# Expert layers: scatter by transposed one-hots, weighing a step ahead of combining, two groups gathered at once; swiglu with the input halves side by side

## The chip, the cores and the metric

One NeuronCore of a Trainium2 chip runs the whole program in one launch. The metric is the device time in microseconds. The kernel before takes 2146.79 us, the median of three runs (2145.88 to 2148.48).

## The reference

Two blocks follow one another, all in fp32, with 256 latent tokens and 256 context tokens of 1024 channels. The first block has two layers, each an attention and Fourier mixer and an expert layer. The second block has one layer: a mixer of two scans, and a swiglu of width 2816.

```python
def expert_choice_ffn(h, w_router, w_gate_e, w_up_e, w_down_e):
    B, N, _ = h.shape
    cap = CAPACITY_FACTOR * N // N_EXPERTS                       # 2 * 256 // 16 = 32
    aff = jax.nn.softmax((h @ w_router).astype(jnp.float32), axis=-1)
    top_aff, top_idx = lax.top_k(aff.transpose(0, 2, 1), cap)    # each expert picks 32 tokens
    bidx = jnp.arange(B)[:, None, None]
    xg = h[bidx, top_idx]
    a = jnp.einsum("becd,edf->becf", xg, w_gate_e)               # 16 experts, 1024 -> 1024
    u = jnp.einsum("becd,edf->becf", xg, w_up_e)
    out = jnp.einsum("becf,efd->becd", jax.nn.silu(a) * u, w_down_e) * top_aff[..., None]
    return jnp.zeros_like(h).at[bidx, top_idx].add(out)

def swiglu(h, w_gate, w_up, w_down):
    return (jax.nn.silu(h @ w_gate) * (h @ w_up)) @ w_down
...
x = x + g2[:, None, :] * expert_choice_ffn(h, w_router[l], w_gate_e[l], w_up_e[l], w_down_e[l])
if need_ctx:                                                     # layer 0 only
    xc = xc + cg2[:, None, :] * expert_choice_ffn(hc, w_router[l], w_gate_e[l], w_up_e[l], w_down_e[l])
```

Layer 0 sends two sets of tokens (latents and context) through its experts, layer 1 one set.

## The kernel before

**Expert layers.** `moe` runs a layer in steps e = 0 to 16. Step e issues `up(e)` (gate and up of expert e, eight loads of 1 MB), the activation, `down(e-1)` (four loads of 1 MB), the transposes `turn(e)`, and then what tables name for that step. The 192 loads of a layer are issued by SyncE, whose queue is in order. They go through a ring of SBUF buffers, and a load waits until TensorE is done with what the buffer held before; it also waits for the load eight before it. All ring buffers bear the name `we` in the rows, and a buffer that leaves the ring keeps that name. `LEAVE` says at which load number a buffer leaves, and `big()` then hands it out to hold other data. The ring of layer 0 shrinks in this way from 19 buffers to 10 at load 92, that of layer 1 from 18 to 5.

The 16 experts are four groups of four. The tokens of a group are gathered by matrix products of the tokens (`xr`) with one-hot matrices `P`: `route` returns `gather(g, k)`, which handles channel block k (of 8) of group g for each set, and writes a 128x128 result per set through ScalarE or VectorE into `xg`. `GATHER` puts the gathers of groups 1, 2 and 3 into steps 3, 5 and 7. The way back is prepared by `scatter_mats` at step 7 (`SCATTER`): for each group and set, two products with selection constants (`cscat`) spread the positions `pos` and affinities `affT` over 128 partitions, and two VectorE operations make the matrix `PT` and the weights `aff` from them, through one PSUM buffer. `combine(g)` at steps 7, 9, 12 and 16 (`COMBINE`) weighs the group's outputs by `aff`, splits them into a high and a low half (`oh`), and multiplies them by `PT`. `moe` writes its calls in this order, but a scheduler interleaves the instructions of each engine by priority; `behind()` lets what is in it start no earlier than what has been issued so far.

**Layer 1** carries side work for the second block: its first projections for the context (`hc,w`, `w,hc`), whose loads share SyncE's queue.

**Swiglu.** For fp32 accuracy a product is done as three products of halves (`mm3`): high by high, high by low, low by high. The inputs are split once (`hl`), the weights per block of 256 columns: `halves` casts on ScalarE (`whi`, L173) and subtracts on VectorE (`wlo`, L174), each in two pieces of 1024 columns. Each of the 11 blocks has gate and up (for each, two column halves j and eight kk, so 48 matmuls 256 wide), tanh, two products, a split, and down (24 matmuls 512 wide).

Of the kernel before, what the change touches and what calls it, by code (L numbers as in the profile page):

```python
# [9 lines left out]
F32 = mybir.dt.float32  # L10
F32R = mybir.dt.float32r
# [8 lines left out]
E = 16  # L20
# [67 lines left out]
def _const_scatter():  # L88
    i = np.arange(128)
    sel4 = np.zeros((128, 2, 4, 128))  # L90
    for s in range(2):
        for g in range(4):
            sel4[s * 16 + 4 * g + i // 32, s, g, i] = 1
    return _pack([("p32", (i % 32)[:, None]), ("sel4", sel4)])
# [18 lines left out]
LEAVE = [dict(B=[44, 68, 68, 20, 20], A=[92] * 4), dict(A=[68, 92, 92, 20, 20], S=[32] * 4, O=[32] * 4)]  # L113
# [4 lines left out]
GATHER = {3: 8, 5: 8, 7: 8}  # L118
# [4 lines left out]
class Kernel:  # L123
# [727 lines left out]
    def route(self, l, S):  # L851
# [7 lines left out]
        aff = rp.tile([128, 2, S, E], F32, name="aff")  # L859
# [10 lines left out]
        self.affT = self.ep.tile([R, 256], F32, name="affT")  # L870
        nc.scalar.copy(self.affT, pt.rearrange("p t n -> p (t n)"))
# [20 lines left out]
        def pick(g):

            for s in range(S):
                P[s] = ep.tile([128, 2, 4, 32], F32, name="P1", bufs=2 * S)
                for t in range(2):
                    nc.vector.tensor_tensor(P[s][:, t], iota, pT[:, t, s, 4 * g:4 * g + 4].unsqueeze(2)
                                            .to_broadcast([128, 4, 32]), op=OP.is_equal)
                    nc.vector.tensor_scalar(P[s][:, t], P[s][:, t], r[:, 2 * s + t:2 * s + t + 1], None, op0=OP.mult)

        def gather(g, k):
            if k == 0:
                pick(g)
            ps = self.psum("pg" if g else "mm", [128, S, 4, 32])
            for s in range(S):
# [1062 lines left out]
```

## Time and profile before

| | |
|---|---|
| median of three runs | 2146.79 us |
| profiled execution: time, span | 2146.93 us, 2145.2 us |
| TensorE busy | 1891.1 us (88%) |
| VectorE, ScalarE busy | 969.2 us (45%), 546.9 us (25%) |
| read from HBM | 598.84 MB, mean 280 GB/s over the span |
| expert loads | 3 x 128 of 1024 KB, median 14.4, 12.2 and 14.4 us from issue to landing |
| mean granted TensorE clock | 0.927 |

The table is an average over stages with different limits. The slices of the span, the windows over single stages and the queue that issues the loads tell more, and the rows below are taken from those.

### The profile page before, as it was taken

What the parts mean: (1) busy time and instruction counts of PE and PEld (TensorE: products, weight loads), DVE (VectorE), ACT (ScalarE), POOL (GpSimd) and SP (SyncE); (2) the same over time, 40 slices, a digit from 0 to 9 for tenths busy, and PEclk for the clock granted to TensorE, in tenths of its full rate; (3) what the DMA queues carried; (4) which work ended last, traced back from release to release, by engine and by line L of the source; (5) the groups of instructions that cost most, each with busy time, mean ns of one, the idle gap of its engine ahead of it and who ended that gap; (6) DMA issues with size and microseconds to landing.
All of it is one profiled execution on the core that took longest, in us unless ns stands there. A gap on an engine that the chain in (4) does not pass through costs nothing. (4 is left out here: it accounts for less than half of the span.)

```text
span 2145.2 us, 31259 instructions
## 1 busy us (share of the span) xinstructions
PE 1891.1 (88%) x13102; PEld 1266.5 (59%) x13102; DVE 969.2 (45%) x1928; ACT 546.9 (25%) x1076; POOL 75.4 (4%) x97
## 2 busy tenths in 40 slices
PE   5989999997999998887899977688876669998998
PEld 3957778894443432223878953354432228897997
DVE  3875668743222332215776632222121037765454
ACT  4144532221011100003354410210100024344342
POOL 0210000000000000000200000000000000100000
PEclk9999999998999999999999988798787769998999
DMA  8755738745999789997315579999899983213451
GB/s 317 276 210 204 280 137 344 305 191 225 394 420 420 314 322 419 421 421 299 116 60 206 198 298 416 419 388 394 365 420 415 419 365 118 99 68 130 177 180 57
DMA packets 85453, 601.93 MB, mean 281 GB/s; under 512 B 10048, under 2 KB 10848, under 8 KB 13376
## 3 DMA queue, kind: packets, MB, share of 16 engines
q1 hardware_dynamic: 82928, 594.15, 69.7%
q10 hardware_dynamic: 1840, 5.46, 0.7%
q8 instruction: 103, 1.69, 0.3%
q0 software_dynamic: 544, 0.32, 0.2%
q14 instruction: 38, 0.31, 0.0%
HBM read 598.84 MB, written 1.05 MB: 280 GB/s over the span
## 5 line engine op out<-in xcount | busy, mean ns | idle before, releaser
L158 PE MATMUL ps<-we 128*32 128x256 f32 (+2 forms) x2400 | 356.5, 526 | 85.5 <-DMA we<-w_up_e_dram 41.2
L158 PEld LDWEIGHTS ps<-we 128*32 128x32 f32 (+2 forms) x2400 | 122.5, 137 | 298.0 <-issue 114.7
L174 DVE TENSOR_TENSOR wlo<-w,whi 128x1024 fp32r<-128x1024 f32 x170 | 205.3, 1220 | 94.3 <-ACT whi L173 93.8
L173 ACT CAST whi<-w 128x1024 fp32r<-128x1024 f32 x170 | 174.2, 1045 | 234.8 <-PE ps L164 142.5
L158 PE MATMUL ps<-we,gT 128*32 128x256 f32 (+1 forms) x1536 | 203.6, 502 | 31.0 <-DMA we<-w_down_e_dram 31.0
L1037 DVE TENSOR_TENSOR we<-ps,we 32x512 f32<-32x512 f32 (+1 forms) x128 | 70.9, 554 | 212.5 <-PE ps L158 202.3
L158 PEld LDWEIGHTS ps<-we,gT 128*32 128x32 f32 (+1 forms) x1536 | 66.3, 127 | 141.9 <-issue 74.4
L163 PE MATMUL ps<-hhi,whi 128*128 128x512 f32 (+1 forms) x384 | 131.3, 342 | 0.1
L164 PE MATMUL ps<-hlo,whi 128*128 128x512 f32 (+1 forms) x384 | 131.3, 342 | 0.0
L165 PE MATMUL ps<-hhi,wlo 128*128 128x512 f32 (+1 forms) x384 | 129.5, 340 | 0.1
L158 PE MATMUL ps<-we,xg 128*32 128x256 f32 (+1 forms) x768 | 100.4, 486 | 5.3 <-DMA we<-w_gate_e_dram 3.7
L1004 DVE TENSOR_TENSOR g<-tanh,ps 128x512 f32<-128x512 f32 (+1 forms) x32 | 17.7, 554 | 186.3 <-PE ps L158 186.2
L163 PE MATMUL ps<-hl,whi 128*128 128x256 f32 x352 | 100.7, 286 | 0.1
L165 PE MATMUL ps<-hl,wlo 128*128 128x256 f32 x352 | 99.8, 285 | 0.0
L164 PE MATMUL ps<-hl,whi 128*128 128x256 f32 x352 | 99.7, 285 | 0.0
L1001 ACT ACTIVATE tanh<-ps 128x512 f32<-128x512 f32 (+1 forms) x32 | 15.7, 490 | 309.7 <-PE ps L158 309.7
L164 PE MATMUL ps<-wlo,hhi 128*128 128x256 f32 x320 | 91.7, 288 | 1.0 <-DVE wlo L174 1.0
L165 PE MATMUL ps<-whi,hlo 128*128 128x256 f32 x320 | 91.7, 290 | 0.3 <-DVE hlo L371 0.3
L163 PE MATMUL ps<-whi,hhi 128*128 128x256 f32 x320 | 91.4, 287 | 0.3 <-ACT whi L173 0.3
L1002 DVE SCALAR_TENSOR_TENSOR tanh<-tanh,ps 128x512 f32<-128x512 f32 (+1 forms) x32 | 17.7, 555 | 163.0 <-ACT tanh L1001 162.8
L158 PEld LDWEIGHTS ps<-P,xr 128*128 128x128 f32 x384 | 52.4, 203 | 59.5 <-issue 27.4
L1012 ACT ACTIVATE gT<-ps 128x512 f32<-128x512 f32 (+1 forms) x32 | 15.7, 490 | 278.5 <-PE ps L169 278.5
(425 smaller groups left out, 3500.8 us busy)
## 6 DMA issues: line engine op xcount, KB each, us to landing
we<-w_gate_e_dram SPq DMA_DIRECT2D x128, 1024.0 KB, 14.4
we<-w_up_e_dram SPq DMA_DIRECT2D x128, 1024.0 KB, 12.2
we<-w_down_e_dram SPq DMA_DIRECT2D x128, 1024.0 KB, 14.4
w<-w_in_dram SPq DMA_DIRECT2D x53, 1024.0 KB, 5.2
w<-w_ada_dram SPq DMA_DIRECT2D x48, 1024.0 KB, 6.0
w<-w_mod_dram SPq DMA_DIRECT2D x24, 1024.0 KB, 6.5
w<-w_out_dram SPq DMA_DIRECT2D x12, 1024.0 KB, 5.6
w<-w_gate_dram SPq DMA_DIRECT2D x11, 1024.0 KB, 4.8
```

The lines of the kernel that those rows point to most:

```text
L158: self.nc.tensor.matmul(ps, l, r, start=first, stop=last)
L163: mm(ps, l[0], r[0], start=first, stop=False)
L164: mm(ps, l[0], r[1], start=False, stop=False)
L165: mm(ps, l[1], r[0], start=False, stop=last)
L173: self.nc.scalar.copy(hi, x)
L174: (eng or self.nc.vector).tensor_tensor(lo, x, hi.bitcast(F32), op=OP.subtract)
L1001: nc.scalar.activation(t, pa[:, :W], AF.Tanh, scale=0.5)
L1002: nc.vector.scalar_tensor_tensor(t, t, 1.0, pa[:, :W], op0=OP.add, op1=OP.mult)
L1004: nc.vector.tensor_tensor(g, t, pu[:, :W], op=OP.mult)
L1012: nc.scalar.activation(gT[e], ps, AF.Copy, scale=0.5)
L1037: nc.vector.tensor_tensor(op[e // 4 % 2][p:p + 32, s, j * W:j * W + W], ps[i, :W], gb[s][i, j * W:j * W + W], op=OP.mult)
```

## The change

In `route`, the one-hots of all groups are kept unscaled (`hot`), and `scaled` makes the scaled matrix `P` for the gather from them. A gather can handle n = 2 groups at once, with a 256 wide `P`. `GATHER` becomes {3: 8, 5: 4, 6: 4}: group 1 alone in step 3, groups 2 and 3 together in steps 5 and 6. One buffer of layer 0 leaves the ring at load 68 and no longer at 92.

`scatter_mats` transposes the one-hots (`ident,hot`) in place of the products with `cscat`, copies them from PSUM by ScalarE and VectorE in turn, and gets the affinities by a product of the one-hots with the softmax (`aff,hot`, 4 columns wide). `combine` is cut in two: `weigh` stays at its step, and the matrix products move into the next step.

In the swiglu the two halves of the input lie side by side (`hx`), so that the high half of a weight is multiplied with both by one matmul 512 wide. The low half of a weight is multiplied with the high half of the input as before. The two halves of the result are added by a ScalarE copy and a VectorE addition for each column half j, and the activation reads that sum (`fspg`, `fstp` in the rows) from SBUF.

```diff
-LEAVE = [dict(B=[44, 68, 68, 20, 20], A=[92] * 4), dict(A=[68, 92, 92, 20, 20], S=[32] * 4, O=[32] * 4)]
+LEAVE = [dict(B=[44, 68, 68, 20, 20], A=[68, 92, 92, 92]), dict(A=[68, 92, 92, 20, 20], S=[32] * 4, O=[32] * 4)]
-GATHER = {3: 8, 5: 8, 7: 8}
+GATHER = {3: 8, 5: 4, 6: 4}
...
+        hot = self.hot = [ep.tile([128, 2, E, 32], F32, name="hot", bufs=S) for _ in range(S)]
+        def pick(g, n):
+            e = slice(4 * g, 4 * g + 4 * n)
...
+                    nc.vector.tensor_tensor(hot[s][:, t, e], iota, pT[:, t, s, e].unsqueeze(2)
+                                            .to_broadcast([128, 4 * n, 32]), op=OP.is_equal)
+        def scaled(g, n):
...
+                    nc.vector.tensor_scalar(P[s][:, t], hot[s][:, t, 4 * g:4 * g + 4 * n],
+                                            r[:, 2 * s + t:2 * s + t + 1], None, op0=OP.mult)
...
+        def gather(g, n, k):
...
+            ps = self.psum("pg" if g else "mm", [128, S, n, 4, 32])
             for s in range(S):
                 for t in range(2):
                     self.mm(ps[:, s], self.X[s][:, t, k * 128:k * 128 + 128],
                             P[s][:, t].rearrange("p e c -> p (e c)"), t == 0, t == 1)
...
+                for i in range(n):
+                    put(g + i, k, s, ps[:, s, i])
...
     def scatter_mats(self, S, big):
...
-                ps = self.psum("sm", [128, 2, 256])
-                self.mm(ps[:, 0], sel4[:R, s, g], self.pos, True, True)
-                self.mm(ps[:, 1], sel4[:R, s, g], self.affT, True, True)
-                nc.vector.tensor_scalar(self.PT[:, g, s], ps[:, 0], self.const("p32"), None, op0=OP.is_equal)
-                j = self.eq.tile([128, 256], F32, name="affj")
-                nc.vector.scalar_tensor_tensor(j, ps[:, 1], 1.0, self.PT[:, g, s].bitcast(F32), op0=OP.mult,
-                                               op1=OP.mult, accum_out=self.aff[:, g, s:s + 1])
+                ps = self.psum("tp", [128, 2, 128])
+                for t in range(2):
+                    h = self.hot[s][:, t, 4 * g:4 * g + 4].rearrange("p e c -> p (e c)")
+                    self.tr(ps[:, t], h)
+                    self.mm(pa[:, g, s], h, self.probs[:, t, s, 4 * g:4 * g + 4], t == 0, t == 1)
+                (nc.vector.tensor_copy if (g + s) % 2 else nc.scalar.copy)(self.PT[:, g, s],
+                                                                         ps.rearrange("p t n -> p (t n)"))
+        own = ep.tile([128, 4 * S, 4], F32, name="affj")
+        nc.vector.tensor_tensor(own, pa.rearrange("p g s e -> p (g s) e"),
+                                self.const("of4").unsqueeze(1).to_broadcast([128, 4 * S, 4]), op=OP.mult)
+        nc.vector.tensor_reduce(self.aff.rearrange("p g s -> p (g s)"), own, axis=AX, op=OP.add)
...
+            if e - 1 in COMBINE:
+                combine(COMBINE.index(e - 1), range(S))
             if e in COMBINE:
-                combine(COMBINE.index(e))
+                g = COMBINE.index(e)
+                for sets in ([range(S)] if g < 3 else [[s] for s in range(S)]):
+                    weigh(g, sets)
+                    if g == 3:
+                        combine(g, sets)
...
-                    ps = self.psum(tag, [128, 2, 256])
+                    s = p.tile([128, 2, 256], F32, name="fs" + tag, bufs=2)
                     for j in range(2):
+                        ps = self.psum(tag, [128, 2, 256])
                         for kk in range(KT):
-                            self.mm3(ps[:, j], [x[:, kk, j * 128:j * 128 + 128] for x in w], [h[:, kk] for h in hl],
-                                     kk == 0, kk == KT - 1)
+                            l = [x[:, kk, j * 128:j * 128 + 128] for x in w]
+                            nc.tensor.matmul(ps, l[0], hx[:, kk], start=kk == 0, stop=False, skip_group_check=True)
+                            nc.tensor.matmul(ps[:, 0], l[1], hx[:, kk, 0], start=False, stop=kk == KT - 1,
+                                             skip_group_check=True)
+                        nc.scalar.copy(s[:, j], ps[:, 1])
+                        nc.vector.tensor_tensor(s[:, j], s[:, j], ps[:, 0], op=OP.add)
```

What this moves on the engines is seen at three places. The first is TensorE in layer 0 around step 7. Before, the products with `cscat` and the first `combine` (`we 128x512`) stand between the end of the gather (`P,xr`) with `down(6)` (`we,gT`) and `up(8)` (`we 64x512`):

```order
L158 MATMUL ps<-we,gT 64x512 x4
L158 MATMUL ps<-P_5600,xr 128x128 x2
L158 MATMUL ps<-pos,cscat 128x256
L158 MATMUL ps<-affT,cscat 128x256
L158 MATMUL ps<-pos,cscat 128x256
L158 MATMUL ps<-affT,cscat 128x256
L158 MATMUL ps<-we 128x512 x6
L158 MATMUL ps<-pos,cscat 128x256
L158 MATMUL ps<-affT,cscat 128x256
L158 MATMUL ps<-we 128x512 x4
```

In the changed kernel, the transposes (`ident,hot`) and the 4-wide products (`aff,hot`) stand inside `down(6)` and the start of `up(8)`, and the first `combine` inside `down(7)`:

```order
L154 MATMUL ps<-aff,hot 128x4 x10
L165 MATMUL ps<-ident,hot 128x128 x2
L154 MATMUL ps<-aff,hot 128x4 x3
L154 MATMUL ps<-we,gT 64x512 x12
L154 MATMUL ps<-we 64x512 x4
L165 MATMUL ps<-ident,hot 128x128 x8
L154 MATMUL ps<-we 64x512
L165 MATMUL ps<-ident,hot 128x128 x2
L154 MATMUL ps<-we 64x512 x27
L165 MATMUL ps<-ident,g 128x128 x4
L154 MATMUL ps<-we,gT 64x512 x4
L154 MATMUL ps<-we 128x512 x5
```

The whole of `up(8)` has moved ahead of the first `combine`, and no gather stands in step 7 any more. The second place is SyncE's queue in layer 1. Before, a load of the second block's `w_in` (`w_12398`) stands between two loads of expert 8's `up`:

```order
L800 DMA we<-w_gate_e_dram 128x2048 x4
L800 DMA we<-w_up_e_dram 128x2048
L1184 DMA w_12398<-w_in_dram 128x2048
L800 DMA we<-w_up_e_dram 128x2048 x3
L800 DMA we<-w_down_e_dram 128x2048 x4
```

In the changed kernel it stands behind the last expert load, with the other loads of `w_in`:

```order
L796 DMA we<-w_up_e_dram 128x2048 x4
L796 DMA we<-w_down_e_dram 128x2048 x8
L1205 DMA w_12315<-w_small_dram 128x384
L1205 DMA w_12317<-w_in_dram 128x2048
L1205 DMA w_12319<-w_in_dram 128x2048
L1205 DMA w_12321<-w_in_dram 128x2048
L1205 DMA w_12323<-w_in_dram 128x2048
L1205 DMA w_12325<-w_in_dram 128x2048
L1205 DMA w_12327<-w_in_dram 128x2048
L1205 DMA w_12329<-w_in_dram 128x2048
```

One load of 1 MB has left the stream of layer 1. The third place is ScalarE in the swiglu, over one block. Before:

```order
L1828 ACTIVATE ft<-ps 128x512
L173 CAST whi<-w 128x1024 x2
L1833 ACTIVATE fghi<-fy 128x512
L173 CAST whi<-w 128x1024 x4
L1828 ACTIVATE ft<-ps 128x512
```

In the changed kernel, where `fspg` and `fstp` are the sums of gate and up:

```order
L1851 COPY fspg<-ps 128x256
L169 CAST whi<-w 128x1024
L1856 ACTIVATE ft<-fspg 128x512
L1851 COPY fstp<-ps 128x256
L169 CAST whi<-w 128x1024
L1851 COPY fstp<-ps 128x256
L169 CAST whi<-w 128x1024
L1861 ACTIVATE fghi<-fspg 128x512
L169 CAST whi<-w 128x1024 x2
L1851 COPY fspg<-ps 128x256
```

Four copies a block stand between the casts that split the weights.

## Rows read from the trace of the kernel before

**Rows 1.** The page, part 2, mean GB/s of the 40 slices of 53.6 us.

```profile
GB/s 317 276 210 204 280 137 344 305 191 225 394 420 420 314 322 419 421 421 299 116 60 206 198 298 416 419 388 394 365 420 415 419 365 118 99 68 130 177 180 57
```

**Rows 2.** The page, part 4, the chain that ended last, share by engine.

```profile
PE 25%; DMA 10%; DVE 3%; issue 3%; ACT 1%; POOL 0%; DVEq 0%; POOLq 0%; ACTq 0%; SPq 0%
```

**Rows 3.** Windows: us, busy PE, PEld, DVE, ACT, POOL, clock, DMA share, GB/s.

```profile
720.00:760.00 40.00, 36.73 (x140) 18.84 (x142) 18.43 (x41) 5.33 (x10) 0.00 (x0) 0.83 0.47 181
```

**Rows 4.** SyncE's queue, 737 to 761 us: start, us, the issues merged.

```profile
737.11 23.33 SPq L800 DMA_DIRECT2D we<-w_down_e_dram  x2
```

**Rows 5.** Waits of SyncE's queue, 700 to 780 us: total, times, longest.

```profile
SPq L800 <- PE ps L158: 53.9, 19, 22.6
```

**Rows 6.** TensorE in order, layer 0: start, us, operation, idle before.

```profile
740.95 1.22 PE L158 MATMUL ps<-pos,cscat 32*128 32x256 f32 x2 [2.18 <-DVE affj L933]
...
759.00 1.94 PE L158 MATMUL ps<-we 128*64 128x512 f32 x8
```

**Rows 7.** Groups by shape, 700 to 770 us: busy, mean ns, idle before.

```profile
L158 PE MATMUL ps<-P,xr 128*128 128x128 f32 x64 | 10.8, 296 | 2.3 <-ACT we L914 1.3 <-DVE we L911 0.9
...
L158 PE MATMUL ps<-we 128*128 128x512 f32 x16 | 7.7, 616 | 0.3 <-DVE xr L1058 0.3
L158 PE MATMUL ps<-pos,cscat 32*128 32x256 f32 x16 | 7.1, 528 | 2.2 <-DVE affj L933 2.2
L158 PE MATMUL ps<-affT,cscat 32*128 32x256 f32 x16 | 5.7, 438 | 0.0
```

**Rows 8.** TensorE, fp32 matmuls 256 wide, two records to each.

```profile
1426.06 7.07 PE L158 MATMUL ps<-w,hc 128*128 128x256 f32 x32
```

**Rows 9.** TensorE, transposes of 128 columns.

```profile
610.90 0.66 PE L169 MATMUL ps<-ident,g 128*128 128x128 f32 x4
```

**Rows 10.** TensorE, fp32 matmuls 8 wide, two records to each.

```profile
1510.18 1.06 PE L158 MATMUL ps<-da,cscan 128*128 128x8 f32 x8
```

**Rows 11.** Window in layer 1, columns as in rows 3.

```profile
1480.00:1520.00 40.00, 35.46 (x263) 20.97 (x262) 12.91 (x32) 4.76 (x11) 0.00 (x0) 0.76 0.77 313
```

**Rows 12.** SyncE's queue, layer 1.

```profile
1484.03 0.42 SPq L1184 DMA_DIRECT2D w<-w_in_dram  x1
1506.86 2.69 SPq L800 DMA_DIRECT2D we<-w_up_e_dram  x3
```

**Rows 13.** Groups of TensorE by shape, 1464 to 1508 us.

```profile
L158 PE MATMUL ps<-hc,w 128*128 128x256 f32 x32 | 9.4, 465 | 0.0
L158 PE MATMUL ps<-P,xr 128*128 128x128 f32 x32 | 6.0, 304 | 2.6 <-DVE we L911 1.5 <-ACT we L914 1.1
...
L158 PE MATMUL ps<-pos,cscat 16*128 16x256 f32 x8 | 3.8, 568 | 1.1 <-DVE affj L933 1.1
```

**Rows 14.** Window behind layer 1, columns as in rows 3.

```profile
1760.00:1768.00 8.00, 4.31 (x18) 3.15 (x19) 4.15 (x11) 4.87 (x10) 1.41 (x2) 0.54 0.42 178
```

**Rows 15.** Window of the swiglu, columns as in rows 3.

```profile
1944.00:2134.00 190.00, 189.89 (x1326) 177.58 (x1326) 96.14 (x106) 73.97 (x88) 0.00 (x0) 0.99 0.41 145
```

**Rows 16.** TensorE in the swiglu: start, us, operation.

```profile
2003.80 0.28 PE L165 MATMUL ps<-hl,wlo 128*128 128x256 f32 x1
...
2005.23 0.28 PE L165 MATMUL ps<-hl,wlo 128*128 128x256 f32 x1
2005.35 0.40 PE L163 MATMUL ps<-whi,fghi 128*128 128x512 f32 x1
...
2006.05 0.40 PE L163 MATMUL ps<-whi,fghi 128*128 128x512 f32 x1
```

**Rows 17.** Groups of the swiglu by shape: busy, mean ns, idle before.

```profile
L174 DVE TENSOR_TENSOR wlo<-w,whi 128x1024 fp32r<-128x1024 f32 x60 | 72.3, 1222 | 66.7 <-ACT whi L173 66.6
...
L173 ACT CAST whi<-w 128x1024 fp32r<-128x1024 f32 x60 | 61.4, 1043 | 100.0 <-PE ps L164 50.1 <-PE ps L165 28.6 <-issue 21.3
...
L1828 ACT ACTIVATE ft<-ps 128x512 f32<-128x512 f32 x11 | 6.5, 593 | 3.8 <-PE ps L165 3.8
...
L371 DVE TENSOR_TENSOR hl<-hf,hl 128x256 fp32r<-128x256 f32 x5 | 2.1, 426 | 0.2
```

More of the change, by code (lines that the diff above doesn't have):

```diff
@@ L89, in _const_scatter @@
     i = np.arange(128)
[L90 to L94, printed above, removed]
+    return _pack([("of4", i[:, None] // 32 == np.arange(4)[None, :])])
 def _const_scan():
@@ L879, in route @@
         nc.vector.tensor_scalar(sel, wk, 0.0, None, op0=OP.is_lt)
-        self.pos = self.ep.tile([R, 256], F32, name="pos")
         nc.vector.tensor_tensor_scan(wk, sel, sel, 0.0, op0=OP.add, op1=OP.max)
-        nc.vector.tensor_tensor(self.pos, wk, sel, op=OP.mult)
-        nc.vector.tensor_scalar(self.pos, self.pos, -1.0, None, op0=OP.add)
+        nc.vector.tensor_tensor(wk, wk, sel, op=OP.mult)
+        nc.vector.tensor_scalar(wk, wk, -1.0, None, op0=OP.add)
         pt = self.psum("sm", [128, 2, S, E])
@@ L901, in gather @@
-        def gather(g, k):
+                    nc.vector.tensor_tensor(hot[s][:, t, e], iota, pT[:, t, s, e].unsqueeze(2)
+                                            .to_broadcast([128, 4 * n, 32]), op=OP.is_equal)
+        def scaled(g, n):
+            for s in range(S):
+                P[s] = ep.tile([128, 2, 8, 32], F32, name="P1", bufs=2)[:, :, :4 * n]
+                for t in range(2):
+                    nc.vector.tensor_scalar(P[s][:, t], hot[s][:, t, 4 * g:4 * g + 4 * n],
+                                            r[:, 2 * s + t:2 * s + t + 1], None, op0=OP.mult)
@@ L902, in gather, with put @@
+        def put(g, k, s, ps):
+            o = self.xg[g][:, k, :, s]
+            if (k + s + g) % 2:
+                nc.vector.tensor_scalar(o, ps, coef[0][:, k, s:s + 1], coef[1][:, k, s:s + 1], op0=OP.mult, op1=OP.add)
+            else:
+                nc.scalar.activation(o, ps, AF.Identity, scale=coef[0][:, k, s:s + 1], bias=coef[1][:, k, s:s + 1])
+        def gather(g, n, k):
             if k == 0:
-                pick(g)
-            ps = self.psum("pg" if g else "mm", [128, S, 4, 32])
+                pick(g, n)
+                scaled(g, n)
+            ps = self.psum("pg" if g else "mm", [128, S, n, 4, 32])
@@ L992, in up @@
                     if gather and i == 0:
-                        gather(0, k)
+                        gather(0, 1, k)
                     for j in range(J):
@@ L1038, in down, with weigh @@
                                             gb[s][i, j * W:j * W + W], op=OP.mult)
-        def combine(g):
-            end = g == 3
+        def weigh(g, sets):
             if g == 0:
                 oh.extend(big(F32R).rearrange("p (s d) -> p s d", s=S) for _ in range(2))
-            for s in range(S):
+            for s in sets:
                 o, hi, lo = op[g % 2][:, s], oh[0][:, s], oh[1][:, s]
@@ L1050, in combine @@
                                                    op0=OP.mult, op1=OP.subtract)
+        def combine(g, sets):
+            end = g == 3
+            for s in sets:
+                hi, lo = oh[0][:, s], oh[1][:, s]
                 for h in range(2):
@@ L1065, in moe @@
         ups = up(0, gather)
-        self.consts(eq, _const_scatter, "cscat", 1 + 512 * S)
-        rest = iter(range(KT, 4 * KT))
+        self.consts(eq, _const_scatter, "cscat")
+        rest = iter([(1, 1, k) for k in range(KT)] + [(2, 2, k) for k in range(KT)])
         for e in range(E + 1):
@@ L1077, in moe @@
             for _ in range(GATHER.get(e, 0)):
-                x = next(rest)
-                if x % KT == 0:
-                    self.xg.append(big().rearrange("p (k e s c) -> p k e s c", k=KT, e=4, s=S))
-                gather(x // KT, x % KT)
+                g, n, k = next(rest)
+                if k == 0:
+                    self.xg.extend(big().rearrange("p (k e s c) -> p k e s c", k=KT, e=4, s=S) for _ in range(n))
+                gather(g, n, k)
             if e == 2:
@@ L1645, in block2 @@
         hp = self.st.enter_context(self.pool("eh", side="left"))
-        room = lambda dtype: [hp.tile([128, KT, 256], dtype, name="hl", tag=x) for x in ("hi", "lo")]
-        hl = room(F32)
+        h = hp.tile([128, 2, KT, 256], F32, name="hl", tag="h")
+        hl = [h[:, 0], h[:, 1]]
         self.queue(["small", 0, 256, 2080, 2336, 2592, 512, 768, 1024, 1280, 1568, 1824, -1, -2, -3, -4],
@@ L1667, in block2 @@
         self.dbg("x2", xs[0])
-        self.swiglu(xs, r, room(F32R))
+        self.swiglu(xs, r, hp.tile([128, KT, 2, 256], F32R, name="hx", tag="h"))
     def mix2(self, p, xs, hl):
@@ L1793, in scans, with swiglu @@
         return o
-    def swiglu(self, xs, r, hl):
+    def swiglu(self, xs, r, hx):
         nc, a, m = self.nc, self.a, self.modT[2]
@@ L1814, in swiglu @@
             for fb in range(F // 256):
-                pss = []
+                sums = []
                 for n, tag in (("w_gate_2", "pg"), ("w_up_2", "tp")):
```

36 lines of the change are left out of this document (11 added, 25 removed).

## Prediction

> **What bounds the kernel now.** I read the slices of the span first. In the expert layers the transfer rate has a roof of about 420 GB/s: it stands at 419 to 421 for slices on end [rows 1]. The chain that ended last goes through TensorE for 25% of the span and through DMA for 10% [rows 2], so where the layers wait, they wait for weights. Time is lost where the rate falls below the roof inside an expert layer. Slices 14 and 15 (layer 0) show 314 and 322, a loss of (106 + 98) / 420 x 53.6 = 26.0 us of transfer. Slices 27 to 29 (layer 1) show 388, 394 and 365, a loss of (32 + 26 + 55) / 420 x 53.6 = 14.4 us [rows 1]. The first and last slices of a layer are mixed with other stages and are left out.
>
> Then I looked for the place. In layer 0 the window of 720 to 760 us moves 181 GB/s [rows 3], which is 239 / 420 x 40 = 22.8 of the 26.0 us. SyncE issues one load at 737.11 and the next at 760.11 (the row's last issue begins 0.33 us before its end) [rows 4], and the longest wait of its queue is 22.6 us, for TensorE [rows 5]. The ring holds 10 buffers there and a layer's first load of `up(8)` is number 8 + 7 x 12 = 92, so load 102 waits until `up(8)` is done with its first buffer. TensorE comes to it only at 759.00 [rows 6]. In layer 1 the ring holds five: load 97 waits for load 92. The window of 1480 to 1520 us moves 313 GB/s [rows 11], a loss of 107 / 420 x 40 = 10.2 us, and SyncE stands from 1484.03 to 1506.86 [rows 12]. The swiglu is bound otherwise: TensorE is busy 189.89 of 190 us at a granted clock of 0.99 [rows 15].
>
> **The change, part by part.** The sums go against the profiled execution's 2146.93 us, 0.14 us from the median.
>
> *Layer 0, ahead of `up(8)`.* Between 700 and 770 us TensorE spends 10.8 us on group 3's gather and idles 2.3 us for its evacuation; 7.1 and 5.7 us on the two selection products of the scatter, with 2.2 us of idle time for the one PSUM buffer (2.18 us of it in one row [rows 6]); and 7.7 + 0.3 us on `combine(0)` [rows 7]. Six of the eight pairs of the scatter stand ahead of `up(8)`: 12.8 x 6/8 + 2.2 = 11.8. So 13.1 + 11.8 + 8.0 = 32.9 us stand in the way. In their place come at most 16 transposes at 0.66 / 4 = 0.165 us [rows 9] and 16 narrow products at 1.06 / 4 = 0.265 us [rows 10], 6.9 us. The double gather has 8 x 4 = 32 matmuls of 256 columns at 7.07 / 16 = 0.442 us [rows 8], 14.1 us, where group 2 alone took about the 13.1 us of group 3: 1.0 us more. Net, TensorE is at `up(8)` some 32.9 - 6.9 - 1.0 = 25 us earlier, at about 735 us, before load 101's issue of old.
>
> That removes the wait that ends last there. Late next are the loads behind `up(7)` and `down(6)`, since steps 5 and 6 now hold the gathers of two groups and the ring still has only 10 buffers; I leave 4 us of the 26.0 there and take a gain of 22 us. Bounds: 26 if nothing is left, and 13 if the 13.1 us of group 3's gather come back as a stall two steps earlier. The earlier leave of one buffer (load 68 for 92) changes the ring from 14 to 13 where the rows show no loss. From there to the end of the layer TensorE is hidden under the transfers (slices 16 to 18 stand at 419 to 421 [rows 1]), so what the stream gains the layer ends earlier. The 16 copies from PSUM are shared by ScalarE and VectorE, which were busy 5.33 and 18.43 of 40 us [rows 3].
>
> *Layer 1, ahead of `up(8)`.* The gather goes (6.0 + 2.6 us), and the `pos` products (3.8 + 1.1 us) with those for the affinities, of the same count and width; eight transposes and eight narrow products come (3.4 us), which I set against the affinity products [rows 13]. That is 13.5 us, and `combine(0)` on top, against 10.2 us lost: all of it should come back. What stays ahead of `up(8)` is the context's projection, 9.4 us [rows 13]. Of the other 4.2 us of the layer's loss I take 2, since part comes from the gather in step 5, which is now longer. Gain 12 us, bounds 8 and 14.4.
>
> *The load that leaves layer 1.* One load of 1.05 MB at 420 GB/s is 2.5 us of that stream. It now comes behind the layer, where the window of 1760 to 1768 us moves 178 GB/s [rows 14] and has room for 242 x 8 = 1.9 MB. I take 2 us; bounds 0 and 2.5.
>
> *Swiglu, TensorE.* Twelve steps of 256 columns take 2003.80 to 2005.23, 0.119 us each; three of 512 take 2005.35 to 2006.05, 0.233 us each [rows 16]. Three of the first are 0.3575 us, one of each is 0.3525: 352 x 0.005 = 1.8 us less. Bounds: 2.8 us less if each 256 columns cost half a 512 step (0.1165 us), and nothing. [...]
>
> *Swiglu, the other engines.* Added are 44 ScalarE copies of 256 columns. ScalarE takes 0.593 us for 512 and 1.043 for 1024 columns [rows 17], so 0.45 less per 512 and about 0.37 for 256: 16.3 us. Added are 44 VectorE additions at 0.426 us [rows 17], 18.7 us. ScalarE goes from 73.97 to about 90 and VectorE from 96.14 to about 115 of 190 us [rows 15], so TensorE covers both on average, and I cost them at nothing. If the cover is gone, a late split costs TensorE a cast and a subtraction, 1.04 + 1.22 = 2.27 us [rows 17].
>
> *The start of a layer* gets one or two VectorE operations ahead of the first gather, 0.3 us in all, with the 0.426 us of rows 17 as the nearest price and 0 to 1 as bounds; the gathers of the later groups lose as many.
>
> Sum: 22 + 12 + 2 + 1.8 - 0.3 = 37.5 us, so 2146.9 - 37.5 = 2109 us.
>
> **The rivals.**
>
> *The stall moves.* The double gathers stand in steps 5 and 6, in front of loads that the same short ring holds back. For it: SyncE's queue waited 19 times for TensorE between 700 and 780 us, not once [rows 5]. Against it: the sum of TensorE's work before `up(8)` falls by 25 us, wherever the gathers stand. Then the lower bounds hold: 13 + 8 + 0 + 0 = 21 us, 2126 us.
>
> *The splits of the swiglu come late.* ScalarE's queue is in program order in the trace, and a copy that waits for TensorE's column half keeps the casts behind it waiting, which the next matrix needs. Place: each of the 22 gate and up matrices. Price: 2.27 us each [rows 17], 50 us. It decides from 37.5 / 22 = 1.7 us a matrix, and by it the time is 2109 + 50 = 2159 us, slower than before. For it: TensorE has no idle time to give there [rows 15], and casts already wait 78.7 us for TensorE in the stage [rows 17]. Against it: those waits are for buffers and cost TensorE nothing; a copy waits for a column half, and the cast behind it has the rest of the block's matmuls ahead of its user. If only the odd blocks are caught, 5 x 2.3 = 11.5 us, 2121 us, inside the range. [...]
>
> *It doesn't do what it says.* The loads wait for another use of TensorE than `up(8)`, and the layers end as before. For it: only the release is inferred from the trace. Against it: 760.11 falls inside the eight records that start at 759.00 [rows 4, 6]. Time: 2147 us.
>
> **How the numbers follow.** The forecast, 2101 to 2118 us (the upper gains of the layers, 26 + 14.4 + 2.5 + 2.8 = 45.7, to a loss of 9 of the 37.5), gets 0.70. The moved stall, 2118 to 2134, gets 0.20, the unchanged time 0.04, the late splits 0.06. The range is 2100 to 2130, which leaves out less than 2 in 10. A measurement of this kernel tells a change of 0.2%, about 4.3 us, from none. The first two cases are faster (0.90), the third is 0.04, the fourth 0.06.
>
> **What would show it.** Right: no window of 40 us inside layer 0 or 1 below 380 GB/s apart from their ends; SyncE's longest wait around load 102 below 8 us; layer 0's last load about 22 us earlier and layer 1's about 36 us; a swiglu that takes TensorE 188 us with no idle time. Wrong: a new dip one or two steps earlier with SyncE waiting for TensorE there (the stall has moved); idle time of TensorE in the swiglu that ends with `whi` or `wlo` (late splits); a rate that still falls to 0 ahead of `up(8)`.

## The result and the profile after

The changed kernel takes 2114.73 us, the median of four runs (2109.1 to 2117.96), against 2147.64 us of the kernel before in the same comparison: ratio 0.9853, 95% interval 0.9834 to 0.9872. The profiled execution took 2116.92 us, its span 2115.1 us, 30.1 us less than before. The forecast was 2109 us, 37.5 us less. Later runs of the same kernel gave 0.9842 (0.9820 to 0.9864).

The slices of the span after (GB/s), which answer to [rows 1], and the chain that ended last, which answers to [rows 2]:

```profile
GB/s 321 279 181 211 271 143 338 293 217 214 376 420 420 372 404 420 420 420 270 116 61 218 189 306 416 418 415 387 393 414 420 419 364 120 102 67 132 179 183 57
```

```profile
PE 70%; DMA 15%; DVE 7%; issue 4%; ACT 3%; POOL 1%; SPq 0%; DVEq 0%; POOLq 0%; ACTq 0%
```

The two chains can't be compared: the shares of [rows 2] add up to 42%, as the chain before could be followed back only to 1221 us, behind layer 0, where the one here goes back to the start of the span. So [rows 2] said nothing of layer 0. The slices 14 and 15 rose from 314 and 322 to 372 and 404: most of layer 0's loss is gone, not all. In layer 1, slices 27 to 29 read 415, 387 and 393 for 388, 394 and 365. Two windows in layer 0, which answer to [rows 3], and then SyncE's queue and its waits, which answer to [rows 4, 5]:

```profile
720.00:760.00 40.00, 36.57 (x178) 15.05 (x174) 9.62 (x18) 5.70 (x11) 0.00 (x0) 0.96 0.88 343
760.00:800.00 40.00, 38.01 (x170) 12.98 (x170) 14.57 (x22) 4.00 (x6) 0.00 (x0) 1.00 1.01 412
```

```profile
733.79 0.33 SPq L796 DMA_DIRECT2D we<-w_up_e_dram  x1
735.51 10.36 SPq L796 DMA_DIRECT2D we<-w_down_e_dram  x4
```

```profile
SPq L796 <- PE ps L154: 71.7, 30, 7.1
```

The window of 720 to 760 us went from 181 to 343 GB/s. SyncE issues the four `w_down` loads 100 to 103 within 10.4 us, where it stood for 22.6 us inside them before; its longest wait is 7.1 us. What is left is a wait ahead of load 103, which is issued at 745.53, 6.6 us behind load 102. TensorE in that place, and the groups by shape of 650 to 770 us, which answer to [rows 6, 7]:

```profile
727.10 2.29 PE L154 MATMUL ps<-aff,hot 128*128 128x4 f32 x20
...
737.01 1.88 PE L154 MATMUL ps<-we 128*64 128x512 f32 x8
740.63 1.65 PE L165 MATMUL ps<-ident,hot 128*128 128x128 f32 x8 [1.73 <-DVE we L938]
...
743.20 0.44 PE L165 MATMUL ps<-ident,hot 128*128 128x128 f32 x2
...
759.04 1.21 PE L154 MATMUL ps<-we 128*128 128x512 f32 x4
```

```profile
L154 PE MATMUL ps<-P,xr 128*128 128x256 f32 x64 | 17.6, 400 | 0.6 <-ACT we L908 0.6
...
L154 PE MATMUL ps<-aff,hot 128*128 128x4 f32 x32 | 4.0, 245 | 0.0
...
L165 PE MATMUL ps<-ident,hot 128*128 128x128 f32 x16 | 3.5, 295 | 1.9 <-DVE we L938 1.7
```

`up(8)` begins at 737.01 and no longer at 759.00, 22.0 us earlier, and the first products of `combine(0)` stand at 759.04, inside `down(7)`. The double gather of two groups takes 17.6 us and idles 0.6.

For layer 1, the window that answers to [rows 11] loses (420 - 366) / 420 x 40 = 5.1 us where 10.2 were lost:

```profile
1460.00:1500.00 40.00, 34.63 (x289) 19.33 (x288) 9.97 (x23) 5.17 (x13) 0.00 (x0) 0.78 0.91 366
```

For the swiglu, the window that answers to [rows 15], and TensorE's steps, which answer to [rows 16]:

```profile
1914.00:2104.00 190.00, 189.55 (x983) 159.38 (x982) 114.12 (x156) 92.19 (x136) 0.00 (x0) 0.98 0.41 144
```

```profile
1984.77 0.40 PE L1848 MATMUL ps<-hx,whi 128*128 128x512 f32 x1
1985.01 0.28 PE L1849 MATMUL ps<-hx,wlo 128*128 128x256 f32 x1
...
1990.43 0.40 PE L1848 MATMUL ps<-hx,whi 128*128 128x512 f32 x1
```

TensorE stays full. Sixteen pairs take 1984.77 to 1990.43, 0.354 us each, and the stage lasts from 1917.5 to 2106.8 us where it lasted from 1944.6 to 2136.8: 192.2 us became 189.2.

To compare kernels, I take the landing times of the 192 expert loads of a layer from the trace, and call the loss between two loads the time between their landings less 2.49 us (1.05 MB at the 421 GB/s of slices 17 and 18 in [rows 1]) for each load. The 30.1 us split so: the last load of layer 0 landed at 990.4 and lands at 972.1 (18.3 us earlier, 17.4 of them between loads 96 and 112), that of layer 1 at 1749.1 and lands at 1722.0 (27.1 us), from there to the swiglu's start it is 195.5 us in both, and the swiglu gives 3.0.

| kernel | ratio to before, 95% interval | layer 0, loads 60-96, 96-112 | layer 1, loads 60-96, 96-112 |
|---|---|---|---|
| before | 1 | -0.1, 25.2 | 12.5, 13.2 |
| changed | 0.9853 (0.9834-0.9872) | 0.4, 7.8 | 9.7, 8.1 |
| changed, once more | 0.9842 (0.9820-0.9864) | 0.0, 6.5 | 9.1, 5.2 |
| without the swiglu's part | 0.9877 (0.9857-0.9896) | 0.6, 7.4 | 9.7, 5.2 |
| without the later combine | 0.9942 (0.9922-0.9963) | -0.1, 16.6 | 9.0, 13.1 |
| without the double gather | 0.9884 (0.9864-0.9905) | 0.5, 9.7 | 11.5, 6.9 |
| without the transposed scatter | 0.9922 (0.9904-0.9940) | 1.1, 13.1 | 8.9, 10.5 |
| later combine alone | 0.9910 (0.9895-0.9925) | 0.0, 13.3 | 9.0, 6.6 |
| transposed scatter alone | 0.9962 (0.9948-0.9975) | -0.1, 17.7 | 12.6, 9.7 |
| gathers in steps 4 and 5 | 0.9864 (0.9848-0.9881) | 6.4, 0.3 | 12.5, 3.0 |
| the same, scatter in step 6 | 0.9874 (0.9857-0.9891) | 15.7, 0.0 | 12.1, 0.9 |
| 40 transposes more in step 7 | 0.9866 (0.9845-0.9888) | 0.1, 12.5 | 8.9, 3.3 |
| 40 transposes more in step 11 | 0.9841 (0.9817-0.9864) | 0.4, 7.6 | 9.0, 1.6 |
| tables per layer | 0.9839 (0.9820-0.9859) | 0.1, 7.8 | 10.1, 0.0 |

(Losses in us, one profiled execution each. Between loads 60 and 96 of layer 1 some 7.5 us in each kernel are three loads of the context's weights; before, and in the kernel without the later combine, the load that has moved is another 2.5 us between loads 96 and 112, which it fills while the queue waits.)

### The profile page after: what moved, and what is told of

It reads as the page before. It is cut to its first block, busy times and chain, and to the rows that moved or that the text cites. A ratio compares the mean times of both kernels' runs of the same rounds, so it can differ in the third digit from the quotient of the medians.

```text
span 2115.1 us, 30458 instructions
## 1 busy us (share of the span) xinstructions
PE 1873.0 (89%) x12678; PEld 1235.5 (58%) x12678; DVE 976.8 (46%) x1934; ACT 564.5 (27%) x1124; POOL 75.4 (4%) x97
## 3 DMA queue, kind: packets, MB, share of 16 engines
HBM read 598.06 MB, written 1.05 MB: 283 GB/s over the span
## 4 chain that ended last, share of the span: by engine, by line
PE 70%; DMA 15%; DVE 7%; issue 4%; ACT 3%; POOL 1%; SPq 0%; DVEq 0%; POOLq 0%; ACTq 0%
PE ps L154 33%; PE ps L161 8%; PE ps L159 8%; PE ps L160 8%; DMA we<-w_down_e_dram 7%; DMA we<-w_up_e_dram 5%; PE ps L165 4%; PE ps L1848 4%; DMA we<-w_gate_e_dram 3%; PE ps L1849 2%; PE ps L268 2%; PE ps L1725 1%; PE ps L313 1%; POOL hr L206 1%; DVE xr L1073 1%
## 5 line engine op out<-in xcount | busy, mean ns | idle before, releaser
L154 PE MATMUL ps<-we 128*32 128x256 f32 (+2 forms) x2400 | 351.2, 528 | 85.8 <-DMA we<-w_up_e_dram 43.4
L1848 PE MATMUL ps<-hx,whi 128*128 128x512 f32 x352 | 125.7, 402 | 0.1
L1849 PE MATMUL ps<-hx,wlo 128*128 128x256 f32 x352 | 98.4, 283 | 0.0
L1011 ACT ACTIVATE tanh<-ps 128x512 f32<-128x512 f32 (+1 forms) x32 | 15.7, 489 | 288.3 <-PE ps L154 288.3
L1022 ACT ACTIVATE gT<-ps 128x512 f32<-128x512 f32 (+1 forms) x32 | 15.7, 490 | 265.4 <-PE ps L165 265.4
L159 PEld LDWEIGHTS ps<-hhi,whi 128*128 128x128 f32 x384 | 73.3, 191 | 9.3 <-issue 1.3
L160 PEld LDWEIGHTS ps<-hlo,whi 128*128 128x128 f32 x384 | 73.3, 191 | 9.3 <-issue 1.9
## 6 DMA issues: line engine op xcount, KB each, us to landing
we<-w_up_e_dram SPq DMA_DIRECT2D x128, 1024.0 KB, 11.4
```

The costliest lines, as they stand in the source:

```text
L154: self.nc.tensor.matmul(ps, l, r, start=first, stop=last)
L159: mm(ps, l[0], r[0], start=first, stop=False)
L160: mm(ps, l[0], r[1], start=False, stop=False)
L1848: nc.tensor.matmul(ps, l[0], hx[:, kk], start=kk == 0, stop=False, skip_group_check=True)
L1849: nc.tensor.matmul(ps[:, 0], l[1], hx[:, kk, 0], start=False, stop=kk == KT - 1, skip_group_check=True)
```

## The experiments

**Each part undone.** Four kernels, each the changed one with one part as before.

```diff
-                            nc.tensor.matmul(ps, l[0], hx[:, kk], start=kk == 0, stop=False, skip_group_check=True)
...
+                            self.mm3(ps[:, j], [x[:, kk, j * 128:j * 128 + 128] for x in w], [h[:, kk] for h in hl],
```

> The changed kernel with the swiglu as before (three matmuls 256 wide, no copies and additions); the expert layers stay changed. Theory (the swiglu's gain is TensorE's, 3.0 us between the traces, of which I forecast 1.8): 2 to 3 us slower than the changed kernel, about 2118 us, and the expert loads land at the same times as in the changed kernel. Rival (the copies cost as much elsewhere as the matmuls save): no difference, 2115 us.

Measured: 2118.91 us, 0.0024 above the changed kernel's ratio, some 5 us, with intervals that overlap; in the trace the stage takes 191.9 us against 189.2. The 2.7 us of the trace are the firmer number. The copies cost nothing that shows.

```diff
-            if e - 1 in COMBINE:
-                combine(COMBINE.index(e - 1), range(S))
...
+                for s in range(S):
+                    weigh(g, [s])
+                    combine(g, [s])
```

> The changed kernel with combine in the same step as weigh, as before. Theory (what counts is TensorE's time ahead of up(8)): combine(0) comes back in front of it, 8.0 us in layer 0 and 4.7 us in layer 1, so 10 to 13 us slower than the changed kernel, about 2126 us, with new waits of SyncE for TensorE around load 102 of layer 0 and 97 of layer 1. Rival (the scheduler fills TensorE anyway, and where combine stands doesn't matter): within 3 us of the changed kernel.

Measured: 2133.1 us, 19 us slower by the ratios, 13.7 us by the spans of the profiled executions (2128.8 against 2115.1). The ratio is above the theory's 10 to 13 us. Layer 0's last load lands 8.8 us later, near the theory's 8.0, and layer 1's another 4.0, near its 4.7. The load of `w_in` stands between loads 96 and 97 again, but it lands at 1485.87, and load 97 is issued only at 1491.58, so it adds nothing there. TensorE in layer 0:

```profile
740.41 3.01 PE L165 MATMUL ps<-ident,hot 128*128 128x128 f32 x10 [3.44 <-DVE we L938]
743.08 4.53 PE L154 MATMUL ps<-we 128*128 128x512 f32 x10
747.95 16.47 PE L154 MATMUL ps<-we 128*128 128x512 f32 x70 [0.33 <-DVE xr L1073]
```

Ten transposes and ten products of `combine` stand in front of `up(8)` (`we` from 747.95 on holds both), with a wait of 3.44 us for the copy that empties PSUM. What stands ahead of `up(8)` counts.

```diff
-GATHER = {3: 8, 5: 4, 6: 4}
+GATHER = {3: 8, 5: 8, 7: 8}
...
+        rest = iter([(g, 1, k) for g in (1, 2, 3) for k in range(KT)])
```

> The changed kernel with single groups gathered in steps 3, 5 and 7 and the table of leaves as before. Theory: group 3's gather comes back ahead of up(8), 13.1 us in layer 0 and 8.6 us in layer 1, less the 1.0 and 2.7 us that the double gather cost in steps 5 and 6: about 12 us in layer 0 and 6 in layer 1, 2132 us. Rival (only TensorE's own saving counts, 17.5 us of single against 14.1 us of double gathers, wherever they stand): 3 to 5 us slower, 2119 us.

Measured: 2118.92 us, 0.0031 above the changed kernel, 7 us with intervals that overlap; 1.9 us more loss in layer 0, not 12. The rival comes nearer. The gather's group in 650 to 770 us, twice that of [rows 7]:

```profile
L154 PE MATMUL ps<-P,xr 128*128 128x128 f32 x128 | 21.3, 296 | 3.3 <-ACT we L908 1.7 <-DVE we L906 1.2
```

Two single groups take 21.3 + 3.3 us, the double one 17.6 + 0.6: 6.4 us apart. TensorE had no wait for loads between the gathers and `up(8)` in layer 0 (its waits there, 0.79 us at most, are for VectorE and ScalarE), so it doesn't matter in which of these steps a gather stands, only how long all of them take together. Not all of the 6.4 us arrive: `up(8)` begins at 740.90, 3.9 us later than in the changed kernel, whose granted clock stands at its lower level for 3.4 us there (0.50 over 730.2 to 733.3 us, 1.00 over 736 to 760) and here does not (1.00 over 720 to 760); and load 103 is issued at 747.58, 2.1 us later, as the changed kernel's wait of 1.73 us for a copy is 0.24 us here.

```diff
+                self.mm(ps[:, 0], sel4[:R, s, g], self.pos, True, True)
+                self.mm(ps[:, 1], sel4[:R, s, g], self.affT, True, True)
+                nc.vector.tensor_scalar(self.PT[:, g, s], ps[:, 0], self.const("p32"), None, op0=OP.is_equal)
```

> The changed kernel with the scatter as before (two products with selection constants for each pair of group and set, two VectorE operations, one PSUM buffer). Theory: ahead of up(8) 11.8 us of the old scatter come in place of at most 6.9 us in layer 0, and about 8 in place of 3.4 us in layer 1: 5 + 4 us slower, 2124 us. Rival (with combine gone from step 7, up(8) has matmuls to fill the waits of the old scatter, and it costs only its own matmuls that stand ahead of up(8)'s first buffer): 0 to 3 us slower, 2116 us.

Measured: 2128.85 us, 15 us slower, more than either. Layer 0 loses 13.1 us between loads 96 and 112 and 4.0 more behind, where the changed kernel lost 7.8 and 1.1. TensorE:

```profile
724.30 0.69 PE L158 MATMUL ps<-pos,cscat 32*128 32x256 f32 x2
...
736.67 0.80 PE L158 MATMUL ps<-pos,cscat 32*128 32x256 f32 x2 [2.16 <-DVE affj L936]
737.26 1.06 PE L158 MATMUL ps<-affT,cscat 32*128 32x256 f32 x2
...
741.86 1.22 PE L158 MATMUL ps<-pos,cscat 32*128 32x256 f32 x2
```

The pairs are late: 2.16 us of waiting for the one PSUM buffer, and the pairs of 741.86 us stand at half the clock (1.22 us where the first takes 0.69). The granted clock is at its lower level from 737.1 to 747.4 us, for 10.2 us where it is 3.4 in the changed kernel.

**Parts alone.** The kernel before with one part of the change. The gathers keep the steps of before, but are written as in the changed kernel.

> The kernel before with combine one step after weigh as the only change. Theory (TensorE's time ahead of up(8) counts microsecond by microsecond): combine(0) goes from in front of up(8), 8.0 us in layer 0 and 4.7 in layer 1: 0.994 of the kernel before. Rival (the parts need each other: the ring's short margin lets a part count only once the others have brought TensorE close to the loads): much less than the 19 us that undoing it cost the changed kernel, 0.998 or more. Second rival (it is combine's place alone that matters): 0.991, the whole of what undoing it cost.

Measured: 2125.79 us, 0.9910. The second rival's number, 19 us: the theory's 12.7 is too low. Layer 0 ends 9.9 us earlier and layer 1 adds 11.1, more than the 4.7 us of its matmuls. The granted clock over the 20 us behind the landing of load 88 is 1.00 where it was 0.74, and the load of `w_in` leaves layer 1 here too; what each of them makes is not shown.

> The kernel before with the scatter by transposed one-hots as the only change; combine and the gathers stay in their steps. Theory: 11.8 us become at most 6.9 us in layer 0 and about 8 become 3.4 us in layer 1: 5 + 4 us, 0.996 of the kernel before. Rival (as undoing it cost 15 us, the old scatter's waits for VectorE count in full): 0.993.

Measured: 2137.56 us, 0.9962 (8 us), near the theory's sum of 9. Its terms fit less well: in the one execution layer 0 gains 8.9 us for 5, and layer 1 2.7 us for 4. The parts do not add up: the two gave 19 and 8 alone, and cost 19 and 15 when undone.

**Where TensorE's time counts.** A dose of dead work, 40 transposes of the identity, in one step or another.

```diff
+            if e == EXTRA:
+                with self.behind():
+                    ps = self.psum("sm", [128, 4, 128])
+                    for i in range(40):
+                        self.tr(ps[:, i % 4], self.ident)
```

> The changed kernel with 40 further transposes of the identity (40 x 0.165 = 6.6 us of TensorE, into PSUM, read by nobody) ahead of the scatter in step 7 of each layer. Theory (what counts is TensorE's time ahead of up(8)): 6 to 7 us slower in layer 0 and 4 to 7 in layer 1, 0.990 to 0.992 of the kernel before, with the loss of transfer between loads 96 and 112 up by as much. Rival (TensorE has slack there by now, and the rest of the loss has another cause): within 2 us of the changed kernel.

> The same 40 transposes in step 11 of each layer. Theory (from layer 0's step 9 on, TensorE is hidden under the transfers, and in layer 1 it waits for loads): no difference from the changed kernel, at most 2 us, 0.985 to 0.986 of the kernel before. Rival (TensorE's time counts wherever it stands): as slow as with the work in step 7.

Measured, beside the changed kernel's 2115.58 us in the same comparison: 2120.11 us with the work in step 7, 2116.23 with it in step 11. The intervals overlap; the traces are clearer. In step 7, the window of layer 0 that read 343 GB/s:

```profile
720.00:760.00 40.00, 38.18 (x197) 17.50 (x194) 9.62 (x17) 5.15 (x10) 0.00 (x0) 0.96 0.80 293
```

The loss between loads 96 and 112 rose from 6.5 and 7.8 in the two executions of the changed kernel to 12.5: 5 to 6 us for 6.6 us of work. Load 102 is issued at 744.32, 5.4 us later than in the changed kernel; the layer's last load lands only 3.3 to 3.7 us later, as load 60 had landed 1.3 to 3.3 us earlier. In step 11 the loss stayed at 7.6. The pieces of the extra work, and the last of the 4-wide products behind them, with `up(8)` from 739.65 us:

```profile
724.75 1.53 PE L166 MATMUL ps<-ident 128*128 128x128 f32 x12
...
738.69 1.03 PE L155 MATMUL ps<-aff,hot 128*128 128x4 f32 x6
```

This shows for layer 0 that TensorE's time ahead of `up(8)` sets the loss, nearly one for one, and that its time three steps later is free. In layer 1 the loss did not rise (3.3 us), and the forecast of 4 to 7 us fell. But the clock was not the same: over the 20 us behind load 88's landing it was granted 1.00, and 0.79 in the changed kernel, and `up(8)` begins 18.2 us behind that landing, where it was 18.5. So layer 1 doesn't tell what the work costs there.

**The rest of layer 0's loss.**

```diff
-GATHER = {3: 8, 5: 4, 6: 4}
+GATHER = {3: 8, 4: 4, 5: 4}
-LEAVE = [dict(B=[44, 68, 68, 20, 20], A=[68, 92, 92, 92]), dict(A=[68, 92, 92, 20, 20], S=[32] * 4, O=[32] * 4)]
+LEAVE = [dict(B=[44, 56, 56, 20, 20], A=[68, 92, 92, 92]), dict(A=[56, 92, 92, 20, 20], S=[32] * 4, O=[32] * 4)]
```

> The changed kernel with the double gathers one step earlier, in steps 4 and 5, and the two buffers that they fill leaving the ring at load 56 in place of 68. Theory of the 7.8 us of transfer that layer 0 still loses between loads 96 and 112: TensorE is behind there because the double gathers of steps 5 and 6 (14.1 us) leave it no step to catch up before the ring is at 10 buffers; with one step more the loss of layer 0 falls below 3 us and the whole gains 4 to 6 us on the changed kernel, 0.983 of the kernel before; layer 1, where TensorE waits for loads again in step 7, stays. Rival (the loss comes from the scatter's place in down(6) and up(8)): no difference.

Measured: 2115.77 us, 0.9864, no gain. The windows say why:

```profile
640.00:680.00 40.00, 39.18 (x169) 17.11 (x167) 9.43 (x20) 7.59 (x16) 0.00 (x0) 1.00 0.95 376
680.00:720.00 40.00, 39.21 (x183) 13.09 (x182) 8.28 (x13) 2.71 (x5) 0.00 (x0) 1.00 0.98 393
720.00:760.00 40.00, 36.16 (x175) 14.99 (x173) 10.71 (x19) 5.70 (x11) 0.00 (x0) 0.96 1.01 418
```

The loss at loads 96 to 112 is gone (0.3 us), and 6.4 us are lost between loads 60 and 96 instead, 376 and 393 GB/s where the changed kernel had 420: the buffers for the gathers left the ring earlier, and the loads now wait there (SyncE's longest wait for TensorE from 640 to 700 us is 7.3 us, 6.3 in the changed kernel). The rival of the moved stall, which I had given the change itself, is what happened to this step.

> The same with the scatter in step 6 as well, its buffer leaving the ring at load 80 in place of 92. Theory of layer 1's rest (8.1 us between loads 96 and 112): the transposes and 4-wide products stand with the context's projection ahead of up(8) and take 5 us there; a step earlier they stand where TensorE waits for loads (1.4 us before each of several), so another 3 to 5 us, 0.981 of the kernel before. Rival (the projection and TensorE's lower clock make the rest, or the buffer given up twelve loads earlier costs as much): no better than the gathers alone.

Measured: 2118.35 us, 0.9874, no gain: layer 0 loses 15.7 us before load 96 and nothing behind it. Load 60 had landed 5.3 us earlier than in the changed kernel, and the last load lands 1.3 us later. In layer 1 the loss behind load 96 fell to 0.9 us.

**Layer 1 with tables of its own.**

```diff
+GATHER = [{3: 8, 5: 4, 6: 4}, {3: 8, 4: 4, 5: 4}]
+SCATTER = [7, 6]
...
+        dict(A=[56, 80, 92, 20, 20], S=[32] * 4, O=[32] * 4)]
```

> The changed kernel with tables of its own for layer 1: double gathers in steps 4 and 5, scatter in step 6, the buffers leaving at loads 56, 80 and 92; layer 0 as changed. Theory (the two layers lose for different reasons: layer 0 moves its loss with its buffers, layer 1 has waiting time for TensorE in steps 6 and 7): layer 1's loss falls as it did with both tables moved, by about 4 us, and layer 0 keeps the changed kernel's: 3 to 4 us faster than the changed kernel run beside it. Rival (4 us are within what one kernel's runs differ, or the earlier leaves cost layer 1 as much): no difference.

Measured: 2114.0 us against 2115.58 of the changed kernel beside it, ratios 0.9839 and 0.9842: the total can't tell them apart. In the trace, layer 1's stretch of 45 us that holds loads 88 to 104 is at the roof, 420 GB/s:

```profile
1458.00:1503.00 45.00, 37.65 (x344) 21.05 (x348) 12.05 (x24) 5.28 (x13) 0.00 (x0) 0.92 1.01 420
```

> The changed kernel once more, unchanged, as the base for the other three on the same chip: 0.985 of the kernel before, 0.983 to 0.987.

Measured: 2115.58 us, 0.9842. Its runs lie between 2108.7 and 2118.1 us, so one execution tells little below 5 us.

## Why the prediction was right

*The mechanism* held in layer 0: the loads waited for TensorE to reach `up(8)`, TensorE now comes there 22.0 us earlier (forecast 25), the rate no longer falls to 0 (0 GB/s over 745 to 760 us before, and now 297 or more in each 4 us from 736 to 760), and SyncE's longest wait is 7.1 us (I had said below 8). No two successive landings around load 102 are more than 4.9 us apart, where two were 23.2 apart. Marks that were missed: two windows of 40 us still read below 380 GB/s, 343 in layer 0 and 366 in layer 1, and layer 1's last load lands 27.1 us earlier, not 36. Undoing the later combine or the transposed scatter brings the loss back (16.6 and 13.1 us between loads 96 and 112 for 7.8), and added work in that place lengthens it by nearly its own time (5 to 6 us for 6.6).

*Layer 0, 22 us forecast, 18.3 measured.* The mis-sized terms are the gather and the scatter. I set the double gather at 32 matmuls by 0.442 us, a start-to-start price, against a group's busy and idle time of 13.1 us; by the same measure it takes 18.2 us for two groups, not 14.1, and saves 6.4 us, not 12. Nor did group 2 take 13.1 us before, as I had it: both groups together took 21.0 + 3.1. The scatter takes 4.0 + 3.5 us and 1.9 of waiting, 9.4, not 6.9. So 6.5 to 7.8 us stay lost where I had left 4. Part of the gain is the clock, of which I said nothing: from 739.9 to 757.0 us it stood at its lower level (0.50 over 750.3 to 756.9) for 13.7 us before, and in the changed kernel for 3.4 us, from 730.0 on.

*Layer 1, 12 us forecast, 5.4 measured in the profiled execution*: 2.8 us between loads 60 and 96, and 10.7 - 8.1 = 2.6 between 96 and 112 (before without the moved load's 2.5 us). In the second execution it was 3.4 + 5.5. I left out two things. The first is that TensorE waits for loads in layer 1's `up(7)`, where the gather of step 7 stood. The last block of `up(7)` and the first of `up(8)`, before and in the changed kernel:

```profile
1478.39 1.07 PE L158 MATMUL ps<-we 128*32 128x256 f32 x16
...
1505.73 4.52 PE L158 MATMUL ps<-we 128*32 128x256 f32 x80
```

```profile
1453.09 1.94 PE L154 MATMUL ps<-we 128*32 128x256 f32 x16 [0.55 <-DMA we<-w_up_e_dram]
...
1474.08 1.07 PE L154 MATMUL ps<-we 128*32 128x256 f32 x16
```

Load 87, which that last block reads, landed at 1475.23 before and lands at 1453.05. So the block began 3.2 us behind its load, and now begins with it, after waits of 4.8 us in four blocks. I had set the 8.6 us of the gather against the loss in full, but only some 3 us of it held TensorE back; the rest stood in time in which TensorE now waits. Of the 13.5 us and `combine(0)` that were to go, 9.5 arrive: `up(8)` begins 18.5 us behind the landing of load 88, and 28.0 before. With the gather back in step 7 (no double gather) it is 19.9, and the loss behind load 96 is 6.9 us, within the 5.2 to 8.1 of the changed kernel.

The second is that TensorE's clock there is not a constant of the kernel: over the 20 us behind load 88's landing it was granted 0.79 and 0.93 in two executions of the same instructions. The changed kernel's TensorE in layer 1, and that of the kernel with work in step 11, which has the same instructions in this stretch:

```profile
1448.10 1.07 PE L154 MATMUL ps<-we 128*32 128x256 f32 x16 [1.40 <-DMA we<-w_up_e_dram]
1450.60 1.94 PE L154 MATMUL ps<-we 128*32 128x256 f32 x16 [1.43 <-DMA we<-w_up_e_dram]
...
1456.80 2.99 PE L154 MATMUL ps<-aff,hot 128*128 128x4 f32 x14
...
1462.11 3.30 PE L154 MATMUL ps<-hc,w 128*128 128x256 f32 x10
...
1474.08 1.07 PE L154 MATMUL ps<-we 128*32 128x256 f32 x16
```

```profile
1446.72 1.93 PE L155 MATMUL ps<-we 128*32 128x256 f32 x16 [1.41 <-DMA we<-w_up_e_dram]
...
1451.70 1.81 PE L155 MATMUL ps<-we 128*32 128x256 f32 x16 [0.56 <-DMA we<-w_up_e_dram]
...
1456.47 1.62 PE L155 MATMUL ps<-aff,hot 128*128 128x4 f32 x14
...
1459.30 2.42 PE L155 MATMUL ps<-hc,w 128*128 128x256 f32 x10
...
1470.39 1.07 PE L155 MATMUL ps<-we 128*32 128x256 f32 x16
```

In the first, the fourteen records of 4-wide products take 2.99 us and ten of `hc,w` 3.30; in the second 1.62 and 2.42. `up(8)` begins at 1474.08 and 1470.39, and the loss is 8.1 and 1.6 us. In both, TensorE waits for expert loads shortly before, and its `up` blocks double from 1.07 to about 1.9 us: the granted clock fell from 1.00 to 0.50 (0.50 over 1451 to 1463 us in the first, and 1.00 over 1465 to 1476), from about 1450 to 1464 us in one, from about 1446 to 1453 in the other. Counted from the landing of load 88, `up(8)` begins after 18.5 and 13.8 us: part of the matmuls ahead of it ran at half the clock. No run sets the clock; this compares executions that differ in it.

*The load that left layer 1*, 2 us forecast. Before, it landed at 1500.15, while load 97 was issued only at 1506.86: it stood inside the wait, and its going alone would have saved nothing. The 2.5 us that I count for it, and take off the wait (10.7 for 13.2), are a way of counting. The stretch from the last expert load to the swiglu is 195.5 us in both executions, 198.2 in the second one of the changed kernel, and 195.5 to 199.8 over all kernels, so what the load costs behind the layer is not shown to within some 3 us.

*Swiglu, 1.8 us forecast, 2.7 to 3.0 measured.* A pair takes 0.354 us, near the 0.3525 worked out. The mis-sized term is the price before: three steps took 0.3595 us, not 0.3575, by 22 such threes in a row.

```profile
1961.02 0.28 PE L163 MATMUL ps<-hl,whi 128*128 128x256 f32 x1
...
1968.93 0.28 PE L163 MATMUL ps<-hl,whi 128*128 128x256 f32 x1
```

That makes 352 x 0.0058 = 2.0 us. The other 0.7 to 1.0 us are not located; the first 16 of these steps, which begin at half the clock (0.50 over 1944.6 to 1948.2 us before and over 1917.5 to 1921.2 after), take 7.46 us before and 7.44 after. TensorE's matmuls did not wait for a split, and its weight loads waited 0.5 us for `whi` and 0.7 us for `wlo` in the whole stage, 0.2 us at most at a time. So the rival of late splits did not happen, though ScalarE's copies waited 26.4 us for TensorE, 4.1 at most, between the casts, with ScalarE at 92.19 and VectorE at 114.12 of 190 us, where I had 90 and 115.

*The start of a layer* cost nothing that shows.

By terms: 18.3 for layer 0, 5.4 + 2.5 for layer 1, 3.0 for the swiglu, and some 0.9 in layer 1's loads ahead of load 60 and behind load 112, 30.1 us. Layer 1 and its load together give 7.9 us of the 14 forecast, at the lower bounds that I had set for them (8 and 0); in the second execution it is 11.4.

## What to carry to other kernels

When loads wait for a buffer that an engine must release, add up that engine's work since it last waited for loads itself: here that sum set the stall (in layer 0, 6.6 us more of it brought 5 to 6 us more loss), and a piece that stood ahead of such waits, as layer 1's gather did, counted for little (some 3 of 8.6 us). Giving buffers away earlier to move the work forward brought the stall forward as well (6.4 us between loads 60 and 96). Compare prices of one kind: a start-to-start step times a count with another such, a group's busy and idle time with another group's.

## What was not expected of the hardware

The same instructions of layer 1 lost 8.1, 5.2 and 1.6 us in three executions (two of the changed kernel, one of the kernel with work in step 11), with a granted clock over the first 20 us behind load 88's landing of 0.79, 0.79 and 0.93. The clock goes with the part of the loss at loads 97 to 100, 5.5, 5.0 and 0.6 us; another 2.6 us of the first stand at its loads 107 and 109. What differed before was the time for which the clock stood at its lower level behind waits of 0.6 to 1.4 us for loads, 13.7, 13.7 and 6.8 us. What decides that time was not settled by these runs.
